# Four activation tiles of a two-layer decoder moved 192 bytes off the weights' place in SBUF

## The chip, the core and the metric

The kernel runs on one core of one Trainium2 chip. The metric is the device time of one launch in microseconds (us); the kernel before has a median of 634.81 us over 3 runs (634.78 to 634.92). The trace is one further execution of the same kernel, taken with the profiler.

## What is computed

One sequence of 256 tokens, 1024 wide, goes through two decoder layers in float32. Each layer normalises the sequence, applies an attention mixer, adds it back, normalises again, applies a squared-ReLU MLP of width 4096 and adds that back. Layer 0 mixes with three groups of 8 heads over dilated windows, layer 1 with 16 heads of causal attention (its one block of 256 keys is the whole sequence).

```
for i in range(DEPTH):                         # 2 layers
    u = rmsnorm(h, norm_mix[i])
    h = h + mixer_i(u)                         # qkv = u @ w_qkv ... @ w_o
    u = rmsnorm(h, norm_ffn[i])
    h = h + jnp.square(jax.nn.relu(u @ w1)) @ w2
```

## The kernel before

All weights (some 112 MB) pass through SBUF once. They come in 200 units of 256 rows by 512 columns. SyncE loads a unit into a `raw` tile (5 buffers). ScalarE then writes `hi`, the weight rounded to the matmul's float32r type (times the norm's gain where there is one), and VectorE writes `lo`, the remainder; `hi` and `lo` have 7 buffers each. Activations are split the same way. A product of a float32 activation with a float32 weight is made of three float32r matmuls (hi with hi, hi with lo, lo with hi), which accumulate in one PSUM tile.

Every matmul has two operands in SBUF: a **stationary** one, 128 rows by 128 columns (512 bytes in each partition), which a weight load (LDWEIGHTS, engine PEld in the profile) puts into the array ahead of the matmul, and a **moving** one of 256 or 512 columns, which then streams through. In this kernel every large matmul has a weight load of its own, and the load for the next matmul runs while the present one streams.

There are four kinds of large matmul, told apart by what they write:

- `acc` (lines 229 to 231, function `mm3`, called by `project`): the projections to q, k and v. Stationary is a 128-column piece of the normalised input's transpose, the tile `u` (`uh` its hi, `ul` its lo); moving are 512 columns of weights. 720 matmuls (432 in layer 0, 288 in layer 1).
- `wo` (the same lines, called by `wo_group`): the output projections. Stationary is the attention output `oh`, `ol`, moving the weights. 144 matmuls.
- `up` (lines 652 to 654, function `up` in `ffn`): the MLP's first product. Here the weights are stationary (128 columns of `hi` or `lo`), and moving are the 256 columns of `uh` or `ul`. 1536 matmuls.
- `y` (lines 229 to 231, called by `down`): the MLP's second product. Stationary is the hidden activation `hh`, `hl`, moving the weights. 768 matmuls.

So `u` takes part in `acc` and in `up`, and in no other matmul. It is held in four tiles of 4 x 256 float32 columns (`uh` and `ul` for each half of the width), written by `norm_transpose` (line 343): TensorE transposes 128-column pieces of `h` into PSUM (`ut`, line 353), ScalarE writes the hi part (line 360), VectorE the lo part (line 361).

The order of the work on each engine is written out by hand: the functions `beat` and `defer` put splits, transposes and softmax pieces between the matmuls at fixed counts. SBUF tiles come from pools, which lie one after the other in the order in which they are made: `lead` (gains and other small tiles), `wp` (`raw`, `hi`, `lo`), `act` (all wide activations, `u` among them), `const` (`h`, identity matrices, the one-column tile `warm`, line 273) and `small` (norm statistics). In the built program the 14 `hi` and `lo` buffers begin at bytes 37,376 to 90,624 of a partition, the four tiles of `u` at 100,864, 104,960, 145,920 and 150,016. All of these are multiples of 512, as are the starts of all other wide tiles.

Of the kernel before, what the change touches and what calls it, by code (L numbers as in the profile page):

```python
# [24 lines left out]
F32 = mybir.dt.float32  # L25
F32R = mybir.dt.float32r
AF = mybir.ActivationFunctionType
# [3 lines left out]
P = 128  # L31
S = 256
# [35 lines left out]
def trunk(ctx, tc, x, rel_bias, norm_mix, norm_ffn, a_w_qkv, a_q_gain, a_k_gain, a_w_o,  # L68
          b_w_qkv, b_q_gain, b_k_gain, b_w_o, ffn_w1, ffn_w2, onehot, mask_a, mask_b, out):
    nc = tc.nc  # L70
# [2 lines left out]
    wp = ctx.enter_context(tc.tile_pool(name="wp", bufs=1))  # L73
    act = ctx.enter_context(tc.tile_pool(name="act", bufs=1))
    const = ctx.enter_context(tc.tile_pool(name="const", bufs=1))
    small = ctx.enter_context(tc.tile_pool(name="small", bufs=6))
    dram = ctx.enter_context(tc.tile_pool(name="dram", bufs=1, space=bass.MemoryType.DRAM))
    ps = ctx.enter_context(tc.tile_pool(name="ps", bufs=1, space=bass.MemoryType.PSUM))
# [2 lines left out]
    def bank(tag, name):  # L81
        return ps.tile([P, 512], F32, tag=tag, bufs=2, name=name)
# [178 lines left out]
    ident = const.tile([P, P], F32, name="ident")  # L261
# [8 lines left out]
                            pattern=[[-1, S + 1]], channel_multiplier=2)  # L270
    mhalf = lead.tile([P, 16], F32, name="mhalf")
    nc.gpsimd.memset(mhalf, -0.5)
    warm = const.tile([P, 1], F32, name="warm")
    nc.scalar.activation(warm, ident[:, 0:1], AF.Exp)

    gt = lead.tile([P, 36], F32, name="gt")
    gqk = {}
# [64 lines left out]
    u = {}  # L342
    rstd = {}

    def norm_transpose(which, half, t, natural):

        if t == 0:
            u[half] = tuple(act.tile([P, 4, S], F32R, tag=f"u{half}{s}", bufs=1, name=f"u{s}_{which}_{half}")
                            for s in ("h", "l"))
        tp = bank("tp", f"ut_{which}_{half}_{t}")  # L350
        for c in range(4):
            k = 4 * half + c
            nc.tensor.transpose(out=tp[:, c * P:(c + 1) * P], in_=h[:, t, k * P:(k + 1) * P], identity=ident)  # L353
        hi, lo = u[half]
        i = tp.rearrange("p (c q) -> p c q", c=4)
        if natural:
            hi, lo = (z.rearrange("p c (q t) -> p t c q", t=NT)[:, t] for z in (hi, lo))
        else:
            hi, lo = (z[:, :, t * P:(t + 1) * P] for z in (hi, lo))
        nc.scalar.activation(hi, i, AF.Copy)  # L360
        nc.vector.tensor_sub(lo, i, hi.bitcast(F32))
# [33 lines left out]
    def norm_half(which, half, natural=False, lead=2):  # L395
        for t in range(NT):
            defer(lead + t, lambda t=t: norm_transpose(which, half, t, natural))
        defer(lead + 3, lambda: norm_squares(which, half))
        if half == 1:
            defer(lead + 7, lambda: norm_scale(which, natural))  # L400
# [287 lines left out]
    for t in range(NT):  # L688
        norm_transpose(0, 0, t, False)
        keep_warm(1)  # L690
        for _ in range(2):
            next_hi()
            next_lo()
    for t in range(NT):
        defer(4 + t, lambda t=t: norm_transpose(0, 1, t, False))
# [96 lines left out]
```

## Time and profile before

| | |
|---|---|
| median of 3 runs | 634.81 us (634.78 to 634.92) |
| the profiled execution's own time | 634.84 us |
| its span, first to last instruction | 633.0 us |
| TensorE matmul (PE) busy | 627.3 us, 99% of the span, 3902 records |
| TensorE weight load (PEld) busy | 545.7 us, 86% |
| VectorE (DVE) busy | 427.1 us, 67% |
| ScalarE (ACT) busy | 385.2 us, 61% |
| GpSimd (POOL) busy | 36.6 us, 6% |
| DMA queue of the loads | 54.6% of 16 engines |
[...]

A matmul's duration in the trace runs from its start to the modelled end of its last column, and the next one starts before that: durations of consecutive matmuls overlap. What a matmul costs the span is the distance from its start to the start of the next one, its **step**; the chain of work that ended last counts in steps. A longer duration by so many ns goes with a longer step by as many.

### The profile page before, as it was taken

Reading aid. Unit: us, or ns where it says so; the run is one execution under the profiler, and the core shown is the slowest. Engines: PE = TensorE matmul, PEld = TensorE weight load, DVE = VectorE, ACT = ScalarE, POOL = GpSimd, SP = SyncE. Lnnn points to the kernel's source line nnn. Section 1 sums busy time; section 2 is a strip of 40 time slices with the busy share of each in tenths; the row PEclk is TensorE's granted clock in tenths of the full one; section 3 lists DMA queues with packets and bytes.
Section 4 is the critical chain, followed back from the end, with each engine's and each line's share of the span. In section 5 each row is a group of like instructions: output and inputs, shape, how many; then the busy total and the mean of one; then the engine's idle time right before and its main releaser. Section 6 shows DMA issues by size and latency. Waiting matters only on the chain.

```text
span 633.0 us, 10380 instructions
## 1 busy us (share of the span) xinstructions
PE 627.3 (99%) x3902; PEld 545.7 (86%) x3902; DVE 427.1 (67%) x767; ACT 385.2 (61%) x742; POOL 36.6 (6%) x23
## 2 busy tenths in 40 slices
PE   8999999999999999999999999999999999999997
PEld 7778887888989989998988877877999899899886
DVE  5877989766875466467547789887776744754651
ACT  6976876675765356346437778786765643653540
POOL 1222230000000000000000322000000000000000
PEclk9999999999999999999999999999999999999999
DMA  7986456423654564574556666463467446635701
GB/s 247 320 217 211 129 196 173 152 100 134 226 174 169 199 227 139 187 246 140 176 179 198 195 186 195 135 195 134 142 207 251 150 160 223 218 130 187 249 17 67
DMA packets 74538, 113.62 MB, mean 180 GB/s; under 512 B 4584, under 2 KB 30504, under 8 KB 74488
## 3 DMA queue, kind: packets, MB, share of 16 engines
q1 hardware_dynamic: 74312, 112.82, 54.6%
q8 instruction: 31, 0.51, 0.3%
q14 instruction: 19, 0.16, 0.1%
q10 hardware_dynamic: 176, 0.14, 0.1%
HBM read 111.81 MB, written 1.13 MB: 178 GB/s over the span
## 4 chain that ended last, share of the span: by engine, by line
PE 98%; DMA 1%; ACT 0%; DVE 0%; issue 0%; DVEq 0%; SPq 0%; ACTq 0%
PE up L654 10%; PE up L653 10%; PE up L652 10%; PE y L230 9%; PE y L229 9%; PE y L231 9%; PE acc_a L229 6%; PE acc_a L230 5%; PE acc_a L231 5%; PE acc_b L229 4%; PE acc_b L231 3%; PE acc_b L230 3%; PE s_a L518 1%; PE o_a L583 1%; PE ut L353 1%; PE wo_b L229 1%
## 5 line engine op out<-in xcount | busy, mean ns | idle before, releaser
L177 DVE SCALAR_TENSOR_TENSOR lo<-raw,gt,hi 128x512 fp32r<-128x512 f32 x248 | 174.5, 745 | 6.9 <-ACT hi L167 6.8
L167 ACT ACTIVATE hi<-raw,gt 128x512 fp32r<-128x512 f32 x248 | 162.9, 713 | 5.0 <-DMA raw<-in_a_w_qkv_dram 2.0
L652 PE MATMUL up<-uh,hi 128*128 128x256 f32 x512 | 145.1, 283 | 0.0
L654 PE MATMUL up<-uh,lo 128*128 128x256 f32 x512 | 144.9, 283 | 0.0
L653 PE MATMUL up<-ul,hi 128*128 128x256 f32 x512 | 144.9, 283 | 0.0
L175 DVE TENSOR_TENSOR lo<-raw,hi 128x512 fp32r<-128x512 f32 x152 | 98.3, 686 | 43.7 <-ACT hi L165 43.3
L165 ACT ACTIVATE hi<-raw 128x512 fp32r<-128x512 f32 x152 | 88.1, 624 | 54.1 <-PE up L653 21.4
L229 PE MATMUL y<-hi,hh 128*128 128x512 f32 x256 | 100.0, 390 | 0.0
L230 PE MATMUL y<-lo,hh 128*128 128x512 f32 x256 | 99.8, 390 | 0.0
L231 PE MATMUL y<-hi,hl 128*128 128x512 f32 x256 | 99.6, 389 | 0.0
L652 PEld LDWEIGHTS up<-uh,hi 128*128 128x128 f32 x512 | 98.2, 192 | 0.6
L653 PEld LDWEIGHTS up<-ul,hi 128*128 128x128 f32 x512 | 98.2, 192 | 0.5
L654 PEld LDWEIGHTS up<-uh,lo 128*128 128x128 f32 x512 | 98.2, 192 | 0.0
L638 DVE TENSOR_TENSOR r<-r 128x512 f32<-128x512 f32 (+1 forms) x36 | 22.7, 631 | 68.5 <-ACT r L636 68.5
L636 ACT ACTIVATE r<-up 128x512 f32<-128x512 f32 (+1 forms) x36 | 19.8, 550 | 76.1 <-PE up L654 75.7
L229 PE MATMUL acc_a<-hi,uh 128*128 128x512 f32 x144 | 60.3, 419 | 0.0
L231 PEld LDWEIGHTS y<-hi,hl 128*128 128x128 f32 x256 | 48.1, 188 | 10.1
L231 PE MATMUL acc_a<-hi,ul 128*128 128x512 f32 x144 | 56.7, 394 | 0.0
L230 PE MATMUL acc_a<-lo,uh 128*128 128x512 f32 x144 | 56.6, 393 | 0.0
L229 PEld LDWEIGHTS y<-hi,hh 128*128 128x128 f32 x256 | 48.1, 188 | 9.6
L230 PEld LDWEIGHTS y<-lo,hh 128*128 128x128 f32 x256 | 48.1, 188 | 9.4
L229 PE MATMUL acc_b<-hi,uh 128*128 128x512 f32 x96 | 40.0, 417 | 0.0
(128 smaller groups left out, 776.6 us busy)
## 6 DMA issues: line engine op xcount, KB each, us to landing
raw<-in_ffn_w_dram SPq DMA_DIRECT2D x128, 512.0 KB, 4.8
raw<-in_a_w_qkv_dram SPq DMA_DIRECT2D x64, 256.0 KB, 4.0
raw<-in_b_w_qkv_dram SPq DMA_DIRECT2D x24, 512.0 KB, 4.5
raw<-in_b_w_o_dram SPq DMA_DIRECT2D x8, 512.0 KB, 4.8
bias_a<-vdram_a SPq DMA_DIRECT2D x20, 128.0 KB, 5.6
raw<-in_a_w_qkv_dram SPq DMA_DIRECT2D x4, 512.0 KB, 6.3
raw<-in_a_w_o_dram SPq DMA_DIRECT2D x4, 512.0 KB
bias_b<-vdram_b SPq DMA_DIRECT2D x8, 256.0 KB, 4.6
```

The source lines that it names most:

```text
L165: nc.scalar.activation(hi, w, AF.Copy)
L167: nc.scalar.activation(hi, w, AF.Copy, scale=gt[:, gain + c:gain + c + 1])
L175: nc.vector.tensor_sub(lo, w, hi.bitcast(F32))
L177: nc.vector.scalar_tensor_tensor(lo, w, gt[:, gain + c:gain + c + 1], hi.bitcast(F32), op0=ALU.mult, op1=ALU.subtract)
L229: nc.tensor.matmul(acc, lhsT=a[0], rhs=b[0], start=first, stop=False)
L230: nc.tensor.matmul(acc, lhsT=a[0], rhs=b[1], start=False, stop=False)
L231: nc.tensor.matmul(acc, lhsT=a[1], rhs=b[0], start=False, stop=last)
L636: defer(1, lambda: nc.scalar.activation(r, banks[b][:, :w], AF.Relu))
L638: defer(3, lambda: nc.vector.tensor_mul(r, r, r))
L652: nc.tensor.matmul(o, lhsT=whi[:, cols], rhs=uh, start=k == 0, stop=False)
L653: nc.tensor.matmul(o, lhsT=whi[:, cols], rhs=ul, start=False, stop=False)
L654: nc.tensor.matmul(o, lhsT=wlo[:, cols], rhs=uh, start=False, stop=k == 7)
```

## The change

A new pool `ut`, which lies between `const` and `small`, takes the four tiles of `u` out of `act`. The tile `warm` in `const`, of which one column is used, is made 33 columns wide.

```diff
     act = ctx.enter_context(tc.tile_pool(name="act", bufs=1))
     const = ctx.enter_context(tc.tile_pool(name="const", bufs=1))
+
+    ut = ctx.enter_context(tc.tile_pool(name="ut", bufs=1))
     small = ctx.enter_context(tc.tile_pool(name="small", bufs=6))
...
-    warm = const.tile([P, 1], F32, name="warm")
-    nc.scalar.activation(warm, ident[:, 0:1], AF.Exp)
+    warm = const.tile([P, 33], F32, name="warm")
+    nc.scalar.activation(warm[:, 0:1], ident[:, 0:1], AF.Exp)
...
-            u[half] = tuple(act.tile([P, 4, S], F32R, tag=f"u{half}{s}", bufs=1, name=f"u{s}_{which}_{half}")
+            u[half] = tuple(ut.tile([P, 4, S], F32R, tag=f"u{half}{s}", bufs=1, name=f"u{s}_{which}_{half}")
                             for s in ("h", "l"))
```

The instructions of all engines stand in the same order as before, with the same shapes; only addresses differ. In the built program `spread`, the last tile of `const` ahead of `warm`, ends 32 bytes past a multiple of 512, and `warm` takes 160 bytes (132, rounded up to 32) in place of 32. So the four tiles of `u` begin at bytes 210,624, 214,720, 218,816 and 222,912, each 192 bytes past a multiple of 512. `hi` and `lo` stay where they were. The tiles of `act` that lay behind `u` move down by 8,192 or 16,384 bytes and stay at multiples of 512, as do `h` and the identity matrices.

## Rows read from the trace of the kernel before

**Rows 1.** The page: busy time by engine, granted clock, the chain by engine.

```profile
PE 627.3 (99%) x3902; PEld 545.7 (86%) x3902; DVE 427.1 (67%) x767; ACT 385.2 (61%) x742; POOL 36.6 (6%) x23
...
PEclk9999999999999999999999999999999999999999
...
PE 98%; DMA 1%; ACT 0%; DVE 0%; issue 0%; DVEq 0%; SPq 0%; ACTq 0%
```

**Rows 2.** The chain that ended last, whole span, shares by line.

```profile
by line: PE up L654 9.7%; PE up L653 9.7%; PE up L652 9.7%; PE y L230 9.2%; PE y L229 9.2%; PE y L231 9.2%; PE acc_a L229 5.6%; PE acc_a L230 5.3%; PE acc_a L231 5.3%; PE acc_b L229 3.7%; PE acc_b L231 3.5%; PE acc_b L230 3.5%; PE s_a L518 
```

**Rows 3.** Instructions by line, TensorE, `up`: count, duration ns min/median/max, first and last start.

```profile
L652 PEld LDWEIGHTS up<-uh,hi x512: 187/192/192, 152.9 to 606.7; 128*128 128x128 f32 x171
L652 PE MATMUL up<-uh,hi x512: 277/283/365, 153.1 to 606.8; 128*128 128x256 f32 x171
...
L653 PE MATMUL up<-ul,hi x512: 279/283/283, 153.2 to 606.9; 128*128 128x256 f32 x171
...
L654 PE MATMUL up<-uh,lo x512: 278/283/288, 153.3 to 607.0; 128*128 128x256 f32 x171
```

**Rows 4.** The same view, `acc` and `y`, lines 229 to 231.

```profile
L229 PEld LDWEIGHTS acc_a<-hi,uh x144: 186/188/334, 7.8 to 135.7; 128*128 128x128 f32 x144
L229 PE MATMUL acc_a<-hi,uh x144: 389/393/796, 7.8 to 135.9; 128*128 128x512 f32 x144
...
L229 PE MATMUL acc_b<-hi,uh x96: 389/389/504, 334.3 to 418.5; 128*128 128x512 f32 x96
...
L230 PEld LDWEIGHTS y<-lo,hh x256: 187/188/192, 177.0 to 628.3; 128*128 128x128 f32 x128
L230 PE MATMUL y<-lo,hh x256: 387/389/398, 177.2 to 628.5; 128*128 128x512 f32 x128
...
L230 PE MATMUL acc_a<-lo,uh x144: 387/389/796, 8.6 to 136.1; 128*128 128x512 f32 x144
...
L230 PE MATMUL acc_b<-lo,uh x96: 387/389/398, 334.5 to 418.7; 128*128 128x512 f32 x96
...
L231 PE MATMUL acc_a<-hi,ul x144: 388/393/632, 9.2 to 136.3; 128*128 128x512 f32 x144
...
L231 PE MATMUL acc_b<-hi,ul x96: 388/393/400, 334.7 to 419.0; 128*128 128x512 f32 x96
```

**Rows 5.** Timeline where `y` gives way to `up`: start us, us, engine, line, operation.

```profile
187.91 0.28 PE L652 MATMUL up<-uh,hi 128*128 128x256 f32 x1
...
188.14 0.28 PE L654 MATMUL up<-uh,lo 128*128 128x256 f32 x1
...
188.62 0.28 PE L652 MATMUL up<-uh,hi 128*128 128x256 f32 x1
```

**Rows 6.** Instructions by line in 92.2 to 93.3 us, `acc` just after transposes.

```profile
L231 PE MATMUL acc_a<-hi,ul 128*128 128x512 f32 x3 | 1.2, 395 | 0.0
L229 PE MATMUL acc_a<-hi,uh 128*128 128x512 f32 x2 | 0.8, 397 | 0.0
L230 PE MATMUL acc_a<-lo,uh 128*128 128x512 f32 x2 | 0.8, 388 | 0.0
```

**Rows 7.** Waits: engine, line, waited for: us in total, times, longest us.

```profile
ACT hi L165 <- PE up L653: 21.4, 14, 1.5
ACT hi L165 <- PE y L231: 18.8, 12, 1.6
...
ACT hi L167 <- DMA raw<-in_a_w_qkv_dram: 2.0, 2, 1.2
```

## The prediction

> **What bounds the kernel now.** I read the page first. [...] Next the chain by line: it shows what one step costs [rows 2]. Each `up` line has 9.7% of 633.0 us for 512 matmuls, 61.4 us / 512 = 120 ns a step. Each `y` line has 9.2% for 256, 58.2 / 256 = 227 ns. The two differ by 256 columns, so 256 columns stream in 107 ns, and of every step, short or long, 120 - 107 = 13 ns are not columns. These 13 ns are all that this change can touch. The `acc` lines average more (5.3% of 633.0 us for 144 is 233 ns), since their stretches are broken up by small matmuls.
>
> Then I asked whether the 13 ns are a constant. They aren't. The instructions by line give the least, the median and the largest duration: an `up` matmul takes 277 to 279 ns at least, 283 in the median [rows 3]; a 512-column one 387 to 389 at least, 389 or 393 in the median and up to 398 or 400 (the larger maxima are matmuls behind a small matmul, or early ones) [rows 4]. The weight loads move too: 186 ns at the least in `acc`, 188 in the median in `acc` and `y`, 192 in the median in `up` [rows 3, 4]. Same shapes, same operands; what differs is how the load and the stream of columns lie to each other in time. The timeline shows it at a boundary: the first two `up` steps behind `y` take 0.23 us together, the next four 0.48, which is 115 ns each and then 120 [rows 5]. Just after transposes the `acc` matmuls still vary, 388 to 397 ns in the mean of a line, against 389 once they have run on undisturbed [rows 6, 4].
>
> My reading: while a matmul streams its moving operand, the next one's load reads its stationary operand, and the two reads get in each other's way to a degree that depends on which places they touch at the same moment. Before the change both reads begin at 0 modulo 512 in every large matmul, at almost the same time. If place counts, this is the start at which they coincide.
>
> **The change, part by part.** No instruction is added, removed or moved on any engine or queue; only addresses differ. The wider `warm` costs nothing: its one written column stays one column. The tiles of `act` and `small` that move keep their instructions, and they are on DVE, ACT and POOL, which are not in the chain [rows 1]. The writes of `u` to other addresses are 16 pairs on ACT and DVE, also hidden under PE. What is left are the matmuls that read `u`:
>
> - `up`: 1536 matmuls with `u` moving, 192 bytes ahead of the weights that are loaded meanwhile.
> - `acc`: 720 with `u` stationary, so the load is 192 bytes ahead of the stream.
> - `y` and `wo`, 768 and 144, read no `u` and should not move.
>
> The trace has no matmul of this kind with an odd offset, so I bound the price by its spread. Gain end: the offset takes every one of them to the least duration of its line. `up`: 512 x 6 (283 to 277) + 512 x 4 + 512 x 5 = 7.7 us [rows 3]. `acc` by medians: 144 x 4 on line 229 of layer 0 (96 of layer 1 are at their least), 240 x 2 on line 230, 240 x 5 on line 231, 2.3 us [rows 4]. Together 10.0 us. Loss end: every one goes to the largest undisturbed duration, 288 for `up` (+5 x 1536 = 7.7 us), 398 for `acc` (+5 x 144, +9 x 336, +5 x 240 = 4.9 us): 12.6 us. In between lies zero. I take the gain end, because in `up`, which has two thirds of the matmuls, the settled state is nearly the worst of its spread (283 of 277 to 288), and its load is the longest (192 against 186 to 188): there an offset in place has more to win than to lose. In `acc` the settled 389 is already near the least, so little comes from it.
>
> The sum: 634.84 us of the profiled execution (its span of 633.0 and 1.8 around it) - 10.0 = **624.8 us**. That execution is within 0.03 us of the median, so the same number stands for the median.
>
> What covers the rest: with PE 2% quicker, the splits must come 2% sooner. ACT waits for PE in its splits (21.4 and 18.8 us in `up` and `y`) far more than for loads (2.0 us) [rows 7], and is busy for 61%, DVE for 67% [rows 1]. If that cover were gone, PE would wait for `lo` at the start of a unit; I price it at nothing.
>
> **The rivals.**
>
> *No effect.* The 13 ns may belong to swapping weights, and their spread to timing alone, whatever the address. For it: the 13 ns are the same for 256 and 512 columns, and settled `up` steps don't waver. Against it: loads differ by 6 ns for the same shape [rows 3, 4]. Time: 634.8 us. [...]
>
> *More gain.* If the reads collide twice in a step now (both begin together, and the load's end meets the stream again) and once with the offset, half of the 13 ns goes in all 2256 matmuls: 2256 x 6.5 = 14.7 us, 620.2 us. If all of it went: 2256 x 13 = 29.3 us, 605.5 us, the floor. For it: the shift is the same in kind for `up` and `acc`. Against it: no row shows a settled step with less than its line's least. [...]
>
> *Slower.* With equal starts the load and the stream settle into a fixed pattern; with the offset they could meet in mid-stream in every step, which holds both up, or never settle. Its place is `up` first: one more step of the size seen between loads (187 to 192, 5 ns) on 1536 matmuls is 7.7 us; in `acc` the unsettled 395 to 397 [rows 6] would become the rule, some 4.9 us. All of it: 647.4 us, about half: 641. It decides from the point at which the `acc` step has lost 2.1 times (1536 / 720) what the `up` step has gained; with `up` 5 ns cheaper, `acc` would have to lose 11 ns, more than its spread, so it needs `up` itself to go up.
>
> **How the numbers follow.** A measurement of this kernel tells 0.2% (1.3 us) from no change. Forecast, `up` and `acc` near their least: 0.40, with 618 to 631 as its own range. More gain: 0.20. No effect: 0.17. Slower: 0.23. Faster is 0.40 + 0.20 = 0.60. The range of 8 in 10 runs from 612 (of the larger gain about 0.08 lies below) to 641 (of the slower case about 0.10 lies above).
>
> **What would show it.** Right: the median of the `up` matmuls falls from 283 to about 278 ns, their share of the chain from 29.1% to about 28.4%, with loads at 187 or 188; `acc` medians fall by 2 to 5 ns; `y` stays at 389. No effect: 283, 192 and 389 as before. More gain: `up` under 277, `acc` under 387. Slower: `up` at 285 or more, or `acc` at 395 and over, with loads over 192. The reasoning as a whole would be wrong if `y` or `wo`, which read no `u`, changed as much as `up`, or if the time moved while the steps of all four stayed: then addresses act through another engine.

## The result, and the profile after

The change took the kernel from 634.87 us (median of 4 runs, 634.78 to 635.20) to 630.38 us (median of 4, 630.28 to 631.23): ratio 0.9931, interval 0.9914 to 0.9949. Faster, inside the range, but by 4.5 us where 10.0 were forecast. The profiled execution took 630.4 us, with a span of 628.6 (before 633.0).

In this kernel the added lines move every line number of TensorE's loops by two: the `up` matmuls are lines 654 to 656, the shared triple of `acc`, `y` and `wo` is 231 to 233. The page first, the lines that answer to [rows 1]:

```profile
PE 623.0 (99%) x3902; PEld 541.2 (86%) x3902; DVE 426.8 (68%) x767; ACT 385.1 (61%) x742; POOL 36.6 (6%) x23
...
PEclk9999999999999999999999999999999999999999
...
PE 97%; DVE 1%; DMA 1%; ACT 0%; issue 0%; DVEq 0%; SPq 0%; ACTq 0%
```

The counts are the same, the granted clock is the same (1.000 in the mean of both spans), PE is still nearly the whole chain. PE's busy time fell by 4.3 us (627.3 to 623.0), the span by 4.4. PE has no more idle time than before (5.6 us of the span, 5.7 before), so the splits kept up. The chain by line, against [rows 2], says where the time went:

```profile
by line: PE up L654 9.5%; PE up L656 9.5%; PE up L655 9.5%; PE y L231 9.2%; PE y L233 9.2%; PE y L232 9.2%; PE acc_a L231 5.7%; PE acc_a L232 5.4%; PE acc_a L233 5.3%; PE acc_b L231 3.4%; PE acc_b L233 3.2%; PE acc_b L232 3.2%; PE s_a L520 
```

`up` went down: 3 x 9.5% of 628.6 is 179.1 us, from 3 x 9.7% of 633.0, 184.2. The share of `acc_b` fell too, but not because its matmuls became shorter: from 410 to 420 us the chain now runs over DVE and ACT instead of PE. The shares are rounded as well, so the sums that follow are made otherwise: for each large matmul, the distance from its start to the start of the next one on PE, added up by kind.

| kind | before, us | after, us | difference |
|---|---|---|---|
| `up` (1536) | 184.51 | 179.71 | -4.80 |
| `acc` (720) | 173.88 | 174.82 | +0.94 |
| `y` (768) | 174.47 | 174.11 | -0.36 |
| `wo` (144) | 35.23 | 35.25 | +0.02 |

These make -4.2 of the span's -4.4 us. The -0.36 of `y`, which reads no `u`, comes from its entry: the first five steps of the `y` unit at 199 us are 233, 236, 228, 233 and 231 ns before, and 226 or 227 after. It returns when the change runs again (174.10 us in e10), and not where `up` keeps its old step (174.47 and 174.48 in e1 and e11). The instructions by line of `up`, against [rows 3]:

```profile
L654 PEld LDWEIGHTS up<-uh,hi x512: 187/188/190, 153.5 to 602.4; 128*128 128x128 f32 x171
L654 PE MATMUL up<-uh,hi x512: 276/281/367, 153.7 to 602.5; 128*128 128x256 f32 x171
...
L655 PE MATMUL up<-ul,hi x512: 276/281/282, 153.8 to 602.6; 128*128 128x256 f32 x171
...
L656 PEld LDWEIGHTS up<-uh,lo x512: 187/192/192, 153.8 to 602.6; 128*128 128x128 f32 x171
L656 PE MATMUL up<-uh,lo x512: 276/281/283, 153.9 to 602.7; 128*128 128x256 f32 x171
```

The median went from 283 to 281, not to 278, and 192 ns remains in the load of one line of three. A median over 512 hides what happened. The lines of two stretches of PE and PEld, one in the second `up` group of layer 0 (166 to 176 us) and one in the third (188 to 198 us), show two patterns:

```profile
L654 PE MATMUL up<-uh,hi 128*128 128x256 f32 x30 | 8.3, 276 | 0.0
...
L655 PEld LDWEIGHTS up<-ul,hi 128*128 128x128 f32 x30 | 5.6, 188 | 0.0
L656 PEld LDWEIGHTS up<-uh,lo 128*128 128x128 f32 x30 | 5.6, 188 | 0.0
...
L656 PE MATMUL up<-uh,lo 128*128 128x256 f32 x29 | 8.1, 281 | 0.0
...
L656 PEld LDWEIGHTS up<-uh,lo 128*128 128x128 f32 x29 | 5.6, 192 | 0.0
L654 PEld LDWEIGHTS up<-uh,hi 128*128 128x128 f32 x29 | 5.4, 188 | 0.0
```

In the first three rows the matmul takes 276 ns and all loads 188; in the last three it takes 281, and the load of line 656 takes 192. By distances from start to start the first pattern is 113.33 ns a step, the second 117.78; before, every group ran at 120.00. Of the 16 `up` groups (8 in each layer) the first two of each layer, which come one behind the other ahead of any `y` unit, have the better pattern; the 12 that follow a `y` unit have the worse. The timeline where `y` gives way to `up`, against [rows 5]: here the step is 0.12 us from the first on, where before it began at 0.115 and then settled at 0.120.

```profile
187.04 0.39 PE L233 MATMUL y<-hi,hl 128*128 128x512 f32 x1
187.27 0.28 PE L654 MATMUL up<-uh,hi 128*128 128x256 f32 x1
187.39 0.28 PE L655 MATMUL up<-ul,hi 128*128 128x256 f32 x1
187.50 0.28 PE L656 MATMUL up<-uh,lo 128*128 128x256 f32 x1
187.62 0.28 PE L654 MATMUL up<-uh,hi 128*128 128x256 f32 x1
```

And `acc` and `y` by line, against [rows 4]: `y` is at 389 as before; the medians of `acc_b` on lines 231 and 232 rose from 389 to 392, that of `acc_a` on line 232 from 389 to 392.

```profile
L231 PE MATMUL acc_b<-hi,uh x96: 388/392/505, 332.2 to 416.7; 128*128 128x512 f32 x96
...
L232 PE MATMUL y<-lo,hh x256: 389/389/395, 176.6 to 624.2; 128*128 128x512 f32 x128
...
L232 PE MATMUL acc_a<-lo,uh x144: 387/392/793, 8.5 to 136.7; 128*128 128x512 f32 x144
...
L232 PE MATMUL acc_b<-lo,uh x96: 387/392/398, 332.4 to 417.0; 128*128 128x512 f32 x96
```

One thing blurs spans by up to 2 us. In every execution the first `acc` matmuls may take 0.6 to 0.8 us instead of 0.39, and their number differs: 3 in the profiled execution of before, 5 in that of the change, 0 to 11 in the runs below, some 0.2 us each or more. A step among them is 426 or 427 ns (9.21 to 9.64 us in the execution of before). Worked out from the settled steps of that execution, 226.67 for `y` and 120.00 for `up`, 256 columns take 106.67 ns, so 512 take 213.33, and 427 ns is twice that (an estimate). In e3, whose 7 long matmuls begin between 8.79 and 11.52 us, the granted clock is lower there: 0.98 in the mean of the first 9 us and 0.99 from 9 to 153 us, 1.00 from 153 to 330 us, and 0.997 over the whole span. A stretch of 3.3 us at half the clock would give that mean (1 - 0.5 x 3.3 / 633.9 = 0.997, an estimate). In the execution of before the view has 1.00 from 8 to 10 us, so there only the step is long. So I compare mean steps (those not broken up by small matmuls: under 150 ns for `up`, 260 for the others) rather than spans.

### The profile page after: what moved, and what is told of

Same layout as the page of the kernel before. It is cut to its first block, busy times and chain, and to the rows that moved or that the text cites. A ratio compares the mean times of both kernels' runs of the same rounds, so it can differ in the third digit from the quotient of the medians.

```text
span 628.6 us, 10380 instructions
## 1 busy us (share of the span) xinstructions
PE 623.0 (99%) x3902; PEld 541.2 (86%) x3902; DVE 426.8 (68%) x767; ACT 385.1 (61%) x742; POOL 36.6 (6%) x23
## 4 chain that ended last, share of the span: by engine, by line
PE 97%; DVE 1%; DMA 1%; ACT 0%; issue 0%; DVEq 0%; SPq 0%; ACTq 0%
PE up L654 10%; PE up L656 9%; PE up L655 9%; PE y L231 9%; PE y L233 9%; PE y L232 9%; PE acc_a L231 6%; PE acc_a L232 5%; PE acc_a L233 5%; PE acc_b L231 3%; PE acc_b L233 3%; PE acc_b L232 3%; PE s_a L520 1%; PE o_a L585 1%; PE ut L355 1%; PE wo_b L231 1%
## 5 line engine op out<-in xcount | busy, mean ns | idle before, releaser
L654 PE MATMUL up<-uh,hi 128*128 128x256 f32 x512 | 143.6, 281 | 0.0
L655 PE MATMUL up<-ul,hi 128*128 128x256 f32 x512 | 143.3, 280 | 0.0
L656 PE MATMUL up<-uh,lo 128*128 128x256 f32 x512 | 143.3, 280 | 0.0
L655 PEld LDWEIGHTS up<-ul,hi 128*128 128x128 f32 x512 | 96.1, 188 | 0.6
L654 PEld LDWEIGHTS up<-uh,hi 128*128 128x128 f32 x512 | 96.1, 188 | 0.5
```

What stands on the lines that cost most here:

```text
L654: nc.tensor.matmul(o, lhsT=whi[:, cols], rhs=uh, start=k == 0, stop=False)
L655: nc.tensor.matmul(o, lhsT=whi[:, cols], rhs=ul, start=False, stop=False)
L656: nc.tensor.matmul(o, lhsT=wlo[:, cols], rhs=uh, start=False, stop=k == 7)
```

## The experiments

Theory: the step depends on the distance between what a matmul streams and what is loaded beneath it, and on nothing else that the change did. Rivals: the place of `u` itself, the pool and the other tiles that moved, or chance. "Distance" below is that of `u` from the weights in bytes; the change has 192, before has 0.

**Same pool, no distance (e1); all tiles moved, no distance (e2).** The first is the change with a wider `warm`, the second the kernel before with one unused tile of 192 bytes ahead of all wide ones.

```diff
-    warm = const.tile([P, 33], F32, name="warm")
+    warm = const.tile([P, 120], F32, name="warm")
```

```diff
+    lead.tile([P, 48], F32, name="pad")
```

> u in a pool of its own as in the change, but at a multiple of 512 (warm is 120 columns wide). Theory D, the distance between u and the weights modulo 512 sets the step: as before the change, 634.8 us, up matmuls 283 ns in the median with loads of 192. Theory M, it is the other tiles that moved (act by 8 or 16 KB, small by some bytes) or the pool itself: as after the change, 630.4 us, up 281 with loads of 188.

> The kernel before with 192 bytes of padding ahead of all wide tiles: every wide tile lies 192 past a multiple of 512, and u and the weights still at the same place to each other. Theory D (distance): 634.8 us, up 283 and loads 192 as before. Theory A (the absolute place of u counts, whatever the weights do): about 630.4 us, up 281; y, whose tiles are now shifted too, then also changes.

Measured: 634.89 us, ratio 0.9998 (0.9986 to 1.0011), and 635.15 us, 1.0005 (0.9994 to 1.0016). `up` has the step of before, 119.91 in the mean, and its rows too (e1, then e2, by line):

```profile
L654 PEld LDWEIGHTS up<-uh,hi x512: 187/192/192, 153.0 to 606.8; 128*128 128x128 f32 x171
L654 PE MATMUL up<-uh,hi x512: 277/283/365, 153.2 to 606.9; 128*128 128x256 f32 x171
```

```profile
L653 PEld LDWEIGHTS up<-uh,hi x512: 187/192/193, 152.8 to 606.7; 128*128 128x128 f32 x171
L653 PE MATMUL up<-uh,hi x512: 277/283/365, 153.1 to 606.8; 128*128 128x256 f32 x171
```

So neither the pool, nor the moved small tiles, nor the place of `u` by itself does it. The distance does.

**Other distances (e3 to e8).** The change with `warm` of another width; a width of w moves `u` by 4 bytes a column.

```diff
-    warm = const.tile([P, 33], F32, name="warm")
+    warm = const.tile([P, 1], F32, name="warm")
```

Widths 1, 56, 24, 32, 48 and 16 give 64, 256, 128, 160, 224 and 96.

> The change with an offset of 64 bytes in place of 192. Theory D with a period of 64: as before, 634.8. Theory D with a period of 128 bytes: as after (192 is 64 modulo 128), 630.4, up 281. Theory D with a period of 512: something else than either, between 624 and 640.

> The change with an offset of 256 bytes in place of 192. Theory D with a period of 64, 128 or 256: as before, 634.8, up 283. Theory D with a period of 512: half a period, the farthest place from 0, 624 to 632 us with up at 277 to 281.

> The change with an offset of 128 bytes. Offsets of 0 and 256 gave the same steps (up 120 ns, acc as before), 64 and 192 others, so the period is taken to be 256 and 128 is the farthest place from 0. Theory D2 (the two reads meet where they touch the same part of 256 bytes; farthest is best): up at most 117 ns a step, 625 to 630 us. Theory P (the period is really 128 for 0, and 64 and 192 differ only by their order): as with 0, 634.8 us, up 120.

> The change with an offset of 160 bytes, 32 short of 192. If 32-byte steps count: up and acc between those of 128 and 192. If only blocks of 64 bytes count: as with 128 (or 192) to a tenth of a ns in the up step.

> The change with an offset of 224 bytes, 32 short of 256. If 32-byte steps count: up step between 117 (at 192) and 120 (at 256). If only blocks of 64 bytes count: as with 192, 630.4 us, up 117, acc as after.

> The change with an offset of 96 bytes. From 64 (up 117.8 and acc 233.5 ns a step, 634.7 us) towards 128: if the loss in acc belongs to the stream running just behind the load, acc falls back towards 229 and the time under 634; if acc stays at 233, the offset's sign decides and not the distance from 0.

| distance | median us | ratio (interval) | `up` step, ns | `acc` step, ns |
|---|---|---|---|---|
| 0 (e1) | 634.89 | 0.9998 (0.9986 to 1.0011) | 119.91 | 229.04 |
| 64 (e3) | 634.70 | 0.9998 (0.9986 to 1.0009) | 117.80 | 233.49 |
| 96 (e8) | 639.17 | 1.0064 (1.0041 to 1.0087) | 120.00 | 233.68 |
| 128 (e5) | 638.05 | 1.0034 (1.0010 to 1.0057) | 119.65 | 232.33 |
| 160 (e6) | 635.68 | 1.0002 (0.9991 to 1.0013) | 118.53 | 233.39 |
| 192 (the change) | 630.38 | 0.9931 (0.9914 to 0.9949) | 116.78 | 229.81 |
| 224 (e7) | 635.18 | 1.0006 (0.9994 to 1.0018) | 118.32 | 232.78 |
| 256 (e4) | 635.16 | 1.0002 (0.9990 to 1.0015) | 119.91 | 229.14 |

Two things follow. At 256 all is as at 0, while 64 and 192 differ: as far as these distances show, the period is 256 bytes, not 128 or 512. And at every other distance between 0 and 256 what `up` wins is lost again in `acc`, whose step rises by 3 to 5 ns: 192 is the only one of these at which `up` wins and `acc` loses little. At 96 and at 128 the kernel is slower, my rival of the other sign in its mildest form. At 96 `up` never settles (steps of 115 to 126 ns alternate) and `acc` is up everywhere. Not all went as expected. The distance of 64 has the time of before only because a gain and a loss cancel. At 128, the farthest place from 0, 625 to 630 us or 634.8 were expected, and 638.05 came. At 160 `acc` lies outside what 128 and 192 have. And neither the distance from 0 nor its sign orders the steps of `acc`. By line in the run at 96, against 283 for `up` and 389 to 393 for `acc` before:

```profile
L231 PE MATMUL acc_b<-hi,uh x96: 391/400/506, 336.2 to 421.7; 128*128 128x512 f32 x96
...
L655 PE MATMUL up<-ul,hi x512: 278/282/290, 155.0 to 610.3; 128*128 128x256 f32 x171
...
L656 PE MATMUL up<-uh,lo x512: 278/282/298, 155.1 to 610.4; 128*128 128x256 f32 x171
```

**The two roles of `u` apart (e9, e11).** In the kernel before, the tiles of `u` get a little more room in a pool of their own (`ut`, between `act` and `const`), and two views of it: e9 takes the view at distance 192 for the norms of the MLP (`up`) and that at 0 for those of attention (`acc`); e11 the reverse. The change itself ran again beside e9 (e10).

```diff
-            u[half] = tuple(act.tile([P, 4, S], F32R, tag=f"u{half}{s}", bufs=1, name=f"u{s}_{which}_{half}")
-                            for s in ("h", "l"))
+            shifted = which % 2 == 1
+            u[half] = []
+            for s, width, at in (("h", 1072, 48 if shifted else 0), ("l", 1104, 0 if shifted else 80)):
+                z = ut.tile([P, width], F32R, tag=f"u{half}{s}", bufs=1, name=f"u{s}_{which}_{half}")
+                u[half].append(z[:, at:at + 4 * S].rearrange("p (c q) -> p c q", c=4))
```

(e11 has `which % 2 == 0`; both put the small tile `rest` in a buffer that is free then, for room.)

> u lies 192 bytes off the weights where the MLP reads it (moving, in up), and at the weights' own place where the projections read it (stationary, in acc): each u tile is made some columns longer and holds both views; the tile rest goes to a buffer of L to make room. If the two roles act apart: up 117 ns a step as in the change (4.8 us off), acc as before the change (0.9 us less than in it), 629.2 to 629.8 us, 0.9 us under the change. If the gain needs both: over 630.4.

> The change itself once more, beside the kernel that shifts u for up alone, on the same chip: 630.4 us.

> The reverse: u 192 bytes off where it is stationary (acc), aligned where it is moving (up). If the two roles act apart: up 120 ns a step, acc as in the change, 634.9 + 0.9 = 635.8 us. If acc loses only because up changed: 634.9.

| kernel | median us | ratio (interval) | `up` step | `acc` step |
|---|---|---|---|---|
| e9, `up` alone | 630.68 | 0.9927 (0.9913 to 0.9941) | 116.78 | 229.09 |
| e10, the change | 630.33 | 0.9929 (0.9916 to 0.9942) | 116.78 | 229.86 |
| e11, `acc` alone | 635.28 | 1.0006 (0.9996 to 1.0016) | 119.91 | 229.87 |

The roles act apart: `up` has the whole gain, and `acc` loses 0.8 ns a step, 720 x 0.8 = 0.6 us. The times alone would not say so. That of e9 lies outside the 629.2 to 629.8 us expected for this, and that of e11 halfway between its two forecasts. The median of e9 doesn't show the 0.6: it is within the spread of e10, and its runs lie between 629.57 and 630.72. Its profiled execution had 8 long `acc` matmuls at the start, that of before 3, which is 1 us the other way. The step of `acc` is what shows it, not the time. The `acc` rows of e9 are those of before again (389 in the median of `acc_b`):

```profile
L230 PE MATMUL acc_b<-hi,uh x96: 389/389/504, 332.6 to 416.9; 128*128 128x512 f32 x96
```

**Which pair of operands? (e12)** Here `u` and `hi` stay at 0, the low parts of the weights move by 64. In a triple of `up` the moved weights belong to the third matmul alone, and are loaded while the second streams. If the load of the next weights meets the stream, the second line should change; if a matmul minds its own weights, the third.

```diff
+            hi = wp.tile([P, 2, 512], F32R, tag="hi", bufs=SPLIT, name=f"hi_{i}")
+            if i == 0:
+                wp.tile([P, 16], F32, name="pad")
+            lo = wp.tile([P, 2, 512], F32R, tag="lo", bufs=SPLIT, name=f"lo_{i}")
+            if i == 0:
+                wp.tile([P, 112], F32, name="pad2")
```

> u at a multiple of 512 as before, the lo weights 64 bytes past one (so that u is 192 past them modulo 256), the hi weights unshifted. In up, the step of line 653 streams ul while the next load reads lo; the step of line 654 streams uh with lo already loaded, while the next load reads hi. Theory C (the stream and the load of the next weights collide): the step of line 653 falls from 120 to about 117, those of lines 652 and 654 stay at 119 to 120; some 1.5 us off up, 632.5 to 634.5 us. Theory O (the place of the stream against its own weights counts): the step of line 654 falls and that of 653 stays.

Measured: 637.0 us, ratio 1.0044 (1.0031 to 1.0057). A miss for both. The steps of `up` come to 117.85 in the mean, those of the three lines lie between 117.5 and 118.3. The expectation had also left out that `acc` and `y` read `lo`: the `y` step rose from 227.2 to 231.98 (+3.6 us), `acc` to 231.64 (+1.6 us), and that outweighs the gain in `up` (-3.2 us).

```profile
L659 PE MATMUL up<-uh,lo 128*128 128x256 f32 x512 | 144.3, 282 | 0.0
L657 PE MATMUL up<-uh,hi 128*128 128x256 f32 x512 | 144.2, 282 | 0.0
L658 PE MATMUL up<-ul,hi 128*128 128x256 f32 x512 | 143.9, 281 | 0.0
L234 PE MATMUL y<-hi,hh 128*128 128x512 f32 x256 | 101.0, 395 | 0.0
...
L659 PEld LDWEIGHTS up<-uh,lo 128*128 128x128 f32 x512 | 98.1, 192 | 0.0
```

These are groups of the page. What is shown: a place changed in one matmul of three changes all three, so the steps are coupled, and `y`, which reads no `u`, changes with the place of `lo`. That one read waits for the other, and which, is not shown.

**Does the entry decide the pattern? (e13, e14)** In the change only the groups behind `y` have 117.78. So the first matmul of those 12 groups gets a transpose of 128 columns ahead of it, into columns that the group then overwrites; e13 in the change, e14, as a control, in the kernel before.

```diff
+                if j >= 2 and c == 0:
+                    nc.tensor.transpose(out=o[:, 0:P], in_=ident, identity=ident)
```

> The change, with one 128-column transpose put ahead of the first matmul of each of the 12 up groups that follow y (it writes where that matmul writes, and is overwritten). Theory E (the way of entry decides): these groups run at 113.3 ns a step in place of 117.8, 12 x 96 x 4.45 = 5.1 us less, and 12 transposes cost 0.11 to 0.25 us each, 1.3 to 3.0 us: 627 to 629 us. Theory F (the pattern belongs to the group's own addresses or to what runs beside it): 117.8 stays, 631.7 to 633.4 us.

> The same 12 transposes in the kernel before (u at the weights' place). At distance 0 up should settle at 120 whatever comes ahead of it: 634.9 + 1.3 to 3.0, 636.2 to 637.9 us, up at 120. If entry alone decides and the distance does not matter: under 634.9, up under 118 in these groups.

Measured: e13 629.40 us, ratio 0.9907 (0.9890 to 0.9923), just above the range of theory E, as only part of the groups followed it. 8 of the 12 groups go to 113.33, 4 (j of 4 and of 6, in each layer; j counts a layer's groups from 0) stay at 117.78. `up` comes to 177.74 us, the transposes' share at its entries included: 2.0 less than in the change, for 12 instructions more. In the control (636.05 us, one execution) every group stays at 120.00. The lines of PE in 189 to 197 us and in 235 to 242 us of e13, then in 189 to 198 us of e14:

```profile
L656 PE MATMUL up<-uh,hi 128*128 128x256 f32 x24 | 6.6, 276 | 0.0
...
L656 PE MATMUL up<-uh,hi 128*128 128x256 f32 x21 | 5.9, 281 | 0.0
```

```profile
L656 PE MATMUL up<-uh,lo 128*128 128x256 f32 x26 | 7.4, 284 | 0.0
L654 PE MATMUL up<-uh,hi 128*128 128x256 f32 x26 | 7.4, 284 | 0.0
```

So at distance 192 there are two patterns that hold for a whole group where no transposes break it up, and what stands ahead of the stream helps to pick one. At distance 0 only one was seen.

**16 bytes either way (e15, e16).** e9 with both views at 52 columns (208 bytes), and at 44 (176). The tiles of `ul` begin 256 bytes past a multiple of 512 here, which by e4 counts as 0.

```diff
-            for s, width, at in (("h", 1072, 48 if shifted else 0), ("l", 1104, 0 if shifted else 80)):
+            for s, width, at in (("h", 1088, 52 if shifted else 0), ("l", 1088, 52 if shifted else 0)):
```

> u shifted for up alone, by 208 bytes in place of 192 (acc at distance 0). If places count in blocks of 32 or 64 bytes: as with 192, up 113.3 and 117.8, 629.5 to 630.7 us. If 16 bytes count: another mean step, between those of 192 (117.0) and 224 (118.3); a step near 113 in all groups, 625 us, would make the distance the cause of what the forecast missed.

> The same with 176 bytes. If blocks of 32 or 64 bytes count: as with 160 (118.6 in up) or 192. If 16 bytes count: between 160 (118.6) and 192 (117.0); near 113 in all groups, 625 us, if the distance is what the forecast missed.

Measured (one execution each): at 208 the `up` step is 119.16 in all groups, against 116.78 at 192; 634.82 us, with 10 long `acc` matmuls at the start. 16 bytes count, but not as expected: the step isn't between those of 192 and 224 but above both. At 176 nothing can be read: 686.0 us, but the granted clock was 0.852 over the whole execution, and `y`, which this edit doesn't touch, was slower by 9% as well (247.9 ns a step). The cores' view of that run:

```profile
core 0: 684.2 us, clock 0.852
```

**Both gains together (e17), and an attempt at the four groups left (e18).** e17 is e9 with e13's transpose. e18 puts two transposes, not one, ahead of the groups that stayed at 117.78 (j of 4 and 6).

```diff
+                    for _ in range(2 if j in (4, 6) else 1):
+                        nc.tensor.transpose(out=o[:, 0:P], in_=ident, identity=ident)
```

> u shifted by 192 for up alone (acc at distance 0) and one transpose ahead of the 12 up groups that follow y. If the parts add up: as the change with the transposes (629.4 us) less the 0.9 us that acc lost, 628.5 us; up steps of 113.3 in 8 of the 12 groups and 117.8 in 4, acc steps as before the change.

> The same with two transposes, in place of one, ahead of the four groups that stayed at 117.8 (the third and the fifth of those behind y in each layer). If the state at entry decides: these too go to 113.3, 4 x 96 x 4.45 = 1.7 us less, four transposes cost 0.4, 627.2 us. If something in these groups holds them at 117.8: 628.9 us.

Measured: e17 **628.07 us**, ratio 0.9883 (0.9868 to 0.9897), the best of all: 6.7 us off the span of before (626.3), of which `up` has 6.8. e18 629.36 us, 0.9907 (0.9890 to 0.9923): worse, and above both of its forecasts. The groups with j of 4 went to 113.33, but those with j of 6 did not, and those with j of 5 and 7, unchanged from e17, fell back to 117.78. The lines of PE in 232 to 242 us (j of 4) and 254 to 264 us (j of 5), of e17:

```profile
L660 PE MATMUL up<-uh,lo 128*128 128x256 f32 x29 | 8.1, 281 | 0.0
...
L660 PE MATMUL up<-uh,lo 128*128 128x256 f32 x31 | 8.6, 276 | 0.0
```

and of e18:

```profile
L660 PE MATMUL up<-ul,hi 128*128 128x256 f32 x29 | 8.0, 276 | 0.0
...
L660 PE MATMUL up<-ul,hi 128*128 128x256 f32 x29 | 8.1, 281 | 0.0
```

The same entry gives another pattern behind another history: a change at one group alters the pattern of a later one, with a `y` unit between them, and one more small matmul did not set a group's pattern by itself.

## Why the prediction was right and wrong

**Right: what can move, and by what.** PE's steps are the span (PE busy for 627.3 of 633.0 us before and 623.0 of 628.6 after, with 98% and 97% of the chain), no other engine took over, and only addresses act: e1 and e2 exclude everything else that the change did, and nearly all of the time is in the matmuls that read `u`. The 13 ns beyond the columns are not a constant of a weight swap: in the better pattern, with a load for each matmul as before, the step is 113.33 in place of 120.00. That 192 wins was partly luck: nothing in the sum singles it out, every distance other than 0 would have won the same 10.0 us by it, and of the others tried in e3 and e5 to e8 none was faster than before (ratios 0.9998 to 1.0064).

**The step that failed: "the offset takes every one of them to the least duration of its line."** It sized `up` at -7.7 and `acc` at -2.3 us; measured -4.80 and +0.94.

- *`up`.* I took a spread seen in passing, 277 to 288, for the set of values that a settled step can have, and gave its least to all. The reason was misread, too: 283 is not nearly the worst of 277 to 288 but its middle, so the rows gave the gain end no preference. There are two settled values at distance 192. Four groups of 96 gain 120.00 - 113.33 = 6.67 ns a step, more than I allowed (276 is below the least that rows of before had); twelve gain 2.22. That is 384 x 6.67 + 1152 x 2.22 = 5.1 us, of which 4.80 were found: the first group of each layer, which transposes break up, gave 0.55 and 0.48 us in place of 0.64, and before's groups don't begin at 120.00 [rows 5]. Had all groups taken the better pattern, it would have been 1536 x 6.67 = 10.2 us. So it was right that the distance acts on the 13 ns; the error was one price for 1536 matmuls, since what a group follows has a part in its pattern. e13 shows that by changing the entry alone.
- *`acc`.* "Already near the least, so little comes from it" was still priced at a gain, but no distance tried brought the step below that of before (229.8 to 233.7 against 229.1). e9 and e11 give +0.8 ns a step for the offset alone, 0.6 us; the rest of +0.94 are about the 2 more long matmuls at the start, 0.4 us.
- *`y` and `wo`.* At 389 ns, with -0.36 us at the entries of `y`, and +0.02 us: nearly as said. In e12, where `lo` moved, the `y` step did change, from 227.2 to 231.98.

**The rivals.** *No effect* falls: same instructions in the same order, only the distance different, 119.91 against 116.78 ns. *More gain*, half of the 13 ns, is what the better pattern has (13.33 down to 6.67 over the 106.67 of 256 columns, which is 226.67 less 120.00, the settled steps of `y` and `up` before), but in 4 groups of 16, and never in `acc`. No group of `up` in any run settled below 113.33. *Slower* is what other distances do: `acc` at up to 400 and `up` never settled is distance 96, though only by 0.64% and with `acc` doing the harm, which I had put second.

**Left open.** That the two reads collide in the memory fits the period of 256 bytes and the loads of 192 ns, but no run shows a collision itself, and e12 couldn't tell the next load from a matmul's own weights. Distance 176, and a way to bring all groups to 113.33, are open too.

## What to carry to other kernels

Where TensorE is the bound and each matmul loads new weights, the address of the moving operand relative to the weights is worth a sweep: here 1.3% lay between the best and the worst distance (0.9931 and 1.0064 of the time before), with the instructions and their order the same, and the roles of one tile want different distances. Compare steps from start to start by group, not medians by line: a median of 281 hid 113.33 and 117.78. And a stretch's pattern may hang on what ran before it, so no sum should give one price to all instances of a line.

## What the runs showed of the hardware that was not expected

- The step of `up` is the same at a distance of 256 bytes as at 0 (119.91), and 16 bytes matter (116.78 at 192, 119.16 at 208).
- The same stream of matmuls has two stable paces at a distance of 192, 113.33 and 117.78 ns. In the change, 14 of the 16 groups keep one of them for all 96 matmuls (276 ns each in 2 groups, 281 in 12); of the two that transposes break up, that of layer 1 began at 117.78 and went on at 113.33 behind them. What stands ahead of a group counts, even across a whole `y` unit (e18: with a second transpose at j of 4 and of 6, the groups with j of 5 and 7 fell from 113.33 to 117.78).
- 512-column matmuls are not moved by the same distances in the same direction: at 64 `up` won 2.1 ns a step (119.91 to 117.80) and `acc` lost 4.4 (229.04 to 233.49). In `acc` the weights are the moving operand, so the moving one lies 64 bytes further than the stationary one, modulo 256, at a distance of 192: there `acc` lost 0.8. Whether the column count or the role of `u` makes the difference is not separated.
- The granted clock was not the same from execution to execution: in e3 0.98 in the first 9 us and 0.99 from 9 to 153 us, with `acc` steps of 0.42 to 0.43 us from 9.38 to 11.94 us, in that of before 1.00 in both stretches. In the profiled executions 0 to 11 of the first `acc` matmuls took 0.6 to 0.8 us. That is a good part of the noise of this kernel: the profiled execution of e6, which had 11, took 637.17 us where the median of e6 is 635.68.
